# One core, two row tiles: tile 1's last products ordered behind tile 0's, a shorter log1p, and a memory projection that is recorded earlier

## The chip, the core and the metric

The kernel runs on one core of a Trainium2 chip. The metric is the device time of one execution in microseconds (us). A core has five engines that run their own instruction streams side by side: PE (TensorE, matrix products; its weight loads are listed apart as PEld), DVE (VectorE), ACT (ScalarE), POOL (GpSimd) and SP (SyncE, which here issues nearly all of the DMA transfers). They meet only at semaphores.

## The reference

A sequence of 256 rows of width 1024 goes through two blocks of two layers each, everything in float32. Cut to what the change touches:

```
# block 1
for layer in range(2):
    hn  = rmsnorm(h, gains[0])
    mix = mixer_ab(hn, ...) if layer == 0 else mixer_c(hn, ...)   # delta rule + mLSTM | windowed attention
    h   = h + rmsnorm(mix, gains[1])
    ff  = square(relu(rmsnorm(h, gains[2]) @ w_up[layer])) @ w_down[layer]
    h   = h + rmsnorm(ff, gains[3])
    h   = h + sigmoid(h @ w_ple_gate[layer]) * (p[layer] @ w_ple[layer])
# block 2
for layer in range(2):
    # five groups of heads, one of them attends to a memory of 256 rows:
    # its keys and values are rmsnorm(memory) @ w_k[layer], which needs nothing of h
    h = h + mixers(rmsnorm(h), memory) @ w_out[layer]
    h = h + (silu(rmsnorm(h) @ fg[layer]) * (rmsnorm(h) @ fu[layer])) @ fd[layer]
```

`softplus` in `mixer_ab` and `log_sigmoid` in both blocks need `log1p(exp(-|y|))`.

## The kernel before

**Tiles and precision.** The 256 rows are two tiles of 128, t = 0 and t = 1. Every weight matrix comes in blocks of up to 1 MB into one of two `raw` buffers. A block is then split into a high and a low part (`hi<-raw`, mostly on ACT, some on DVE; `lo<-raw,hi` on DVE), in four buffers of `hi` and four of `lo` (`NHL = 4`). A product of float32 accuracy is three PE products: activations high by weight high, high by low, low by high (`nmm`, for outputs with rows on the partitions; `tmm` for transposed outputs). Accumulators are PSUM banks of 512 columns, `ps` in the profile; tile t's result of 1024 columns takes two banks.

**Streams.** `stream` walks over a list of (block, tile) pairs. `lagged(n, lag)` lets tile 1 follow tile 0 by some blocks; `tail_lagged(n, tail)` interleaves the tiles block by block and then does the last `tail` blocks of tile 0 ahead of those of tile 1. At the last block of a tile it calls `done`, which starts a chain on DVE and ACT: for an output projection the sum of squares, the norm and the residual add into `h0` or `h1`, then transposes on PE (`ps<-cf,h`, `ps<-cf,w`) of the new rows, which the next matrix needs as its operand. `w0o` and `w1o` are the output projections of block 1's mixers, `wu`/`wd` the two matrices of its feed-forward (`ff1`), `wg` the gate that follows it, `wi` and `wm` the input projections of block 2's mixers, `wk` the memory's keys and values, `wo` the output projections, `fg`, `fu`, `fd` block 2's feed-forward (`ff2`).

**What sets the order.** No engine call is made at once. A `Recorder` notes all operations of the program with their tiles, derives the dependences from them, gives each a price in nanoseconds from a table, and lists them by a planner that follows the dependences (`order`, `arrange`, `tails`); then each engine's instructions are issued in that order, which the chip keeps. `LAG[a][b]` is the table's delay from an operation of engine a to a dependent one of engine b. `op.preds` are an operation's predecessors. The recording order itself (which the `Loom`, a set of generators, weaves) breaks ties and sets which buffer a tile gets. All of it is recorded by one line, so the profile shows every instruction under L613.

**Where the memory stands.** `memory_rms()` computes the norm of the memory's rows, `memory(0, memory_T(0))` streams the two 1 MB blocks of `wk0` (48 products of 512 columns) and starts the norm and the transposes of the keys. In the kernel before, both are recorded behind block 1's last feed-forward, `ff1(1, ...)`, and ahead of block 2's first mixers.

**log1p.** In `gates` (once, 128x256) and in `forget` (once a layer of block 2, 8 columns) log1p(e) is ln(u) · e / (u − 1) with u = e + 1, and e where u − 1 rounds to zero: seven DVE operations behind the `Ln`, a `RECIPROCAL` among them.

Of the kernel before, what the change touches and what calls it, by code (L numbers as in the profile page):

```python
# [257 lines left out]
class Recorder:  # L258
# [7 lines left out]
           "act": {"pe": 271, "act": 160, "dve": 142, "pool": 155, "sp": 1220},  # L266
           "dve": {"pe": 270, "act": 128, "dve": 127, "pool": 155, "sp": 1220},
           "pool": {"pe": 200, "act": 90, "dve": 69, "pool": 97, "sp": 1220},
           "sp": dict.fromkeys(("pe", "act", "dve", "pool", "sp"), 2050)}

    def __init__(self, nc):
        self.engines = {"pe": nc.tensor, "act": nc.scalar, "dve": nc.vector, "pool": nc.gpsimd, "sp": nc.sync}
        self.ops, self.pools, self.tile_pool, self.seen = [], {}, {}, {}
        self.run = None


    @contextmanager
    def together(self, share=1):

        self.run = []  # L280
        yield
        op = self.ops[self.run[0]]
        op.cost = op.cost / share + 200 * (share > 1)
        self.run = None

    def engine(self, name):
        rec = self
# [53 lines left out]
    def note(self, eng, call, args, kwargs):  # L341
        op = Op()
        op.eng, op.call, op.args, op.kwargs = eng, call, args, kwargs
        op.preds, op.succs, op.tiles, op.alt, op.more = {}, [], [], None, []
        op.table = self.TABLES.get(args[2], 0) if call == "activation" and args[2] != AF.Copy else None
        isap = lambda x: hasattr(x, "tensor") or hasattr(x, "tag_meta")
        outs = [kwargs[k] for k in ("out", "accum_out") if k in kwargs and isap(kwargs[k])]
        ins = [v for k, v in kwargs.items() if k not in ("out", "accum_out") and isap(v)]
        rest = [a for a in args if isap(a)]
        if "out" not in kwargs:  # L350
            outs.append(rest.pop(0))
        op.cost, op.lag = self.price(op, outs[-1], rest + ins), self.LAG[eng]
        if self.run:
            i = self.run[0]
            first = self.ops[i]
            first.more.append((call, args, kwargs))
            first.cost += op.cost
            op = first
        else:
            i = len(self.ops)  # L360
            self.ops.append(op)
            if self.run is not None:
                self.run.append(i)
        for x, write in [(x, False) for x in rest + ins] + [(x, True) for x in outs]:
            for b in self.boxes(x):
                self.touch(i, op, b, write)
# [294 lines left out]
def program(ctx, tc, A, out, dbg=None):  # L661
# [157 lines left out]
    def stream(name, items, acts, kpb, halves_, n, seq, done, before=None):  # L819
# [3 lines left out]
        for t in range(2):  # L823
            for i, tt in seq:
                if tt == t:
                    first.setdefault((items[i][0], t), i)
                    last[items[i][0], t] = i
        banks, live = {}, {}
        w = halves_ * n
        for i, t in seq:  # L830
            c, b, k0 = items[i]
# [5 lines left out]
                banks[c, t] = [acc() for _ in range(halves_)]  # L837
            hi, lo = live[i]
            for j in range(kpb):
                nmm(banks[c, t], acts(t, k0 + j), hi[:, j, :], lo[:, j, :],  # L840
                    first[c, t] == i and j == 0, last[c, t] == i and j == kpb - 1, n)
                if (j + 1) * 3 * halves_ % 6 == 0:
                    loom.step()
            if last[c, t] == i:
                done(c, t, banks.pop((c, t)))

    def a_T(t, k):
# [251 lines left out]
    def mixer_ab(end):  # L1099
        nab = gain(14)  # L1100
        done = {}
        st = {}

        def gates(bank):
# [6 lines left out]
            act.activation(e, e, AF.Exp)  # L1111
            dve.tensor_scalar(u, e, 1.0, None, op0=OP.add)
            act.activation(ln, u, AF.Ln)
            dve.tensor_scalar(u, u, -1.0, None, op0=OP.add)
            dve.scalar_tensor_tensor(z, u, 0.0, e, op0=OP.is_equal, op1=OP.mult)
            dve.tensor_scalar(u, u, 1e-30, None, op0=OP.max)
            dve.reciprocal(u, u)
            dve.tensor_tensor(ln, ln, e, op=OP.mult)
            dve.tensor_tensor(ln, ln, u, op=OP.mult)
            dve.tensor_tensor(ln, ln, z, op=OP.add)  # L1120
            dve.scalar_tensor_tensor(ln, y, 0.0, ln, op0=OP.max, op1=OP.add)
            ca = small(1)
            act.activation(ca, col("alog"), AF.Exp)
# [314 lines left out]
            loom.join(*([("B", j - 2)] if j >= 2 else [("A", j, t)]))  # L1438

        items = [(0, j, 2 * j) for j in (2, 3, 0, 1)]  # L1440
        stream("w0o", items, lambda t, k: done[k // 2, t](k % 2), 2, 2, 512, tail_lagged(4, 2), end, before)


    def mixer_c(r, end):
# [32 lines left out]
        def nat_done(c, t, banks):  # L1477
# [2 lines left out]
        items = [(c, 2 * c + i, 4 * i) for c in (2, 0, 1) for i in range(2)]  # L1480
        stream("w1n", items, a_T, 4, 1, 512, lagged(6, 2), nat_done)
        items = [(0, j, 2 * j) for j in range(4)]
        stream("w1o", items, lambda t, k: done[k // 2, t](k % 2), 2, 2, 512, tail_lagged(4, 2), end,
               lambda it, t: loom.join(("C", it[1], t)))


# [209 lines left out]
    def mixers2(l, r, e, mem, tab, lam, end):  # L1696
# [70 lines left out]
        def forget():  # L1767
# [5 lines left out]
            act.activation(e, e, AF.Exp)  # L1773
            dve.tensor_scalar(u, e, 1.0, None, op0=OP.add)
            act.activation(ln, u, AF.Ln)
            dve.tensor_scalar(u, u, -1.0, None, op0=OP.add)
            dve.scalar_tensor_tensor(z, u, 0.0, e, op0=OP.is_equal, op1=OP.mult)
            dve.tensor_scalar(u, u, 1e-30, None, op0=OP.max)
            dve.reciprocal(u, u)
            dve.tensor_tensor(ln, ln, e, op=OP.mult)  # L1780
            dve.tensor_tensor(ln, ln, u, op=OP.mult)
            dve.tensor_tensor(ln, ln, z, op=OP.add)
            dve.scalar_tensor_tensor(lg, y, 0.0, ln, op0=OP.min, op1=OP.subtract)
            yield
            yield
# [292 lines left out]
    def out1(c, t, banks):  # L2078
# [3 lines left out]
            g2.append(gain(6))  # L2082
        loom.spawn(pre_ff1(1, t, banks, g1[0], g2[0], e, gbo[0]), ("pre", 1, t))

    mixer_c(rc, out1)
    loom.drain()
    dumph("m1")
# [8 lines left out]
        yield from scaled_T(t, gi[0], ri, ei)  # L2096

    ff1(1, e, per_layer_input(1), into2)
    memory_rms()
    mem = memory(0, memory_T(0))  # L2100
    tab, lam = rope_tables2(0)
    loom.drain()
    dumph("f1")
# [57 lines left out]
```

## Time and profile before

| | |
|---|---|
| runs, median (lowest to highest) | 1399.25 us (1395.28 to 1400.75), 3 runs |
| the profiled execution | 1395.2 us, of which the span of the profile is 1393.4 us |
| mean granted clock of TensorE | 0.996 |
| busy share of the span | PE 98%, PEld 86%, DVE 72%, ACT 56%, POOL 4% |
| DMA | 236.36 MB, mean 170 GB/s |

The profile is of one execution; its span leaves 1.8 us of the execution's time outside. An engine's idle time stands in brackets behind the instruction that ended it, with what released it. An operation's row in the timeline has its start, its busy time and how many equal ones followed one another; products are pipelined, so they start closer together than they last.

### The profile page before, as it was taken

The numbers are of one execution on the slowest core, as the hardware profiler recorded it, in microseconds if no ns is written. First come the engines' busy times: TensorE is split into PE (matmuls) and PEld (weight loads), VectorE is DVE, ScalarE is ACT, GpSimd is POOL, SyncE is SP. The second block draws the span as 40 slices with busy tenths as digits, with TensorE's granted clock in tenths as the row PEclk, the third lists the DMA queues.
The fourth block names the chain that finished last, engine by engine and source line by source line (L and its number), as shares of the span: only waits on it lengthen the run. The fifth ranks groups of instructions, "written<-read, shape, count | busy, mean of one in ns | idle before, by whom it ended". The sixth has DMA issues, their size and how long they took to land.

```text
span 1393.4 us, 23108 instructions
## 1 busy us (share of the span) xinstructions
PE 1359.3 (98%) x8768; PEld 1199.4 (86%) x8774; DVE 998.3 (72%) x2417; ACT 786.4 (56%) x1800; POOL 56.4 (4%) x93
## 2 busy tenths in 40 slices
PE   6999999999999999999999999999999999999998
PEld 6899889999787799998787877999998877899997
DVE  6994876666677876566789798575767999576664
ACT  6665554444554854445576596454546679364443
POOL 0000210000010010000020000000001000000000
PEclk9999999999999999999999999999999999999999
DMA  8332354445543364445555243454545523345553
GB/s 329 134 126 99 114 212 182 182 184 194 212 147 141 139 224 179 185 182 194 207 193 206 91 142 132 152 211 153 212 155 205 187 90 99 144 153 210 182 189 114
DMA packets 36400, 236.36 MB, mean 170 GB/s; under 512 B 4160, under 2 KB 4416, under 8 KB 10176
## 3 DMA queue, kind: packets, MB, share of 16 engines
q1 hardware_dynamic: 36288, 234.88, 46.4%
q8 instruction: 69, 1.13, 0.3%
q14 instruction: 43, 0.35, 0.1%
HBM read 233.82 MB, written 1.05 MB: 169 GB/s over the span
## 4 chain that ended last, share of the span: by engine, by line
PE 88%; DVE 6%; ACT 4%; issue 1%; DMA 1%; SPq 0%; POOLq 0%; POOL 0%; ACTq 0%; DVEq 0%
PE ps L613 88%; ACT w L613 3%; DVE w L613 3%; DVE s L613 2%; DMA cf<-in_cf 1%; DVE lo L613 1%; ACT hi L613 1%; DVE h L613 0%; ACT L613 0%; SPq L613 0%; POOLq L2157 0%; DVE hi L613 0%; ACT aTh L613 0%; POOL s L613 0%; ACTq L613 0%
## 5 line engine op out<-in xcount | busy, mean ns | idle before, releaser
L613 ACT ACTIVATE hi<-raw 128x512 fp32r<-128x512 f32 (+1 forms) x793 | 437.6, 620 | 297.7 <-PE ps L613 244.9
L613 DVE TENSOR_TENSOR lo<-raw,hi 128x512 fp32r<-128x512 f32 (+1 forms) x844 | 526.0, 678 | 51.4 <-ACT hi L613 48.1
L613 PE MATMUL ps<-hi,w 128*128 128x512 f32 (+1 forms) x1272 | 379.1, 395 | 0.5 <-ACT w L613 0.5
L613 PE MATMUL ps<-aTl,hi 128*128 128x256 f32 x1256 | 316.7, 280 | 0.0
L613 PE MATMUL ps<-aTh,hi 128*128 128x256 f32 x1256 | 316.3, 281 | 0.0
L613 PE MATMUL ps<-aTh,lo 128*128 128x256 f32 x1256 | 312.5, 280 | 0.0
L613 PEld LDWEIGHTS ps<-hi,w 128*128 128x128 f32 x1272 | 225.2, 188 | 36.1 <-issue 1.9
L613 PEld LDWEIGHTS ps<-aTh,hi 128*128 128x128 f32 x1256 | 224.8, 188 | 9.4 <-ACT hi L613 0.4
L613 PEld LDWEIGHTS ps<-aTl,hi 128*128 128x128 f32 x1256 | 225.1, 188 | 8.3 <-issue 0.4
L613 PEld LDWEIGHTS ps<-aTh,lo 128*128 128x128 f32 x1256 | 223.6, 189 | 9.9 <-DVE lo L613 1.0
L613 PE MATMUL ps<-lo,w 128*128 128x512 f32 (+1 forms) x636 | 205.9, 393 | 0.0
L613 ACT ACTIVATE w<-ps 128x512 f32<-128x512 f32 (+3 forms) x261 | 128.3, 535 | 130.4 <-PE ps L613 119.9
L613 PE MATMUL ps<-hi,aTh 128*128 128x512 f32 (+2 forms) x480 | 148.4, 366 | 3.7 <-ACT w L613 2.5
L613 DVE CAST hi<-raw 128x512 fp32r<-128x512 f32 x51 | 21.8, 427 | 177.8 <-PE ps L613 177.8
L613 PE MATMUL ps<-lo,aTh 128*128 128x512 f32 (+2 forms) x480 | 147.2, 365 | 0.0
L613 PE MATMUL ps<-hi,aTl 128*128 128x512 f32 (+2 forms) x480 | 147.2, 365 | 0.0
L613 ACT ACTIVATE w<-w 128x512 fp32r<-128x512 f32 (+5 forms) x143 | 74.9, 535 | 95.3 <-DVE w L613 93.0
L613 PEld LDWEIGHTS ps<-lo,w 128*128 128x128 f32 x636 | 112.6, 188 | 17.0 <-issue 0.8
L613 PE MATMUL ps<-cf,w 128*128 128x128 f32 (+1 forms) x572 | 94.7, 279 | 17.4 <-DMA cf<-in_cf 10.6
L613 PE MATMUL ps<-w,w 128*64 128x128 f32 (+10 forms) x912 | 109.5, 299 | 0.6 <-ACT w L613 0.5
L613 PEld LDWEIGHTS ps<-w,w 128*128 128x128 f32 (+4 forms) x912 | 88.7, 171 | 20.0 <-ACT w L613 7.4
L613 PEld LDWEIGHTS ps<-hi,aTh 128*128 128x128 f32 x480 | 86.8, 190 | 16.2 <-ACT w L613 2.8
(105 smaller groups left out, 1143.8 us busy)
## 6 DMA issues: line engine op xcount, KB each, us to landing
raw<-in_wu SPq DMA_DIRECT2D x32, 1024.0 KB, 4.8
raw<-in_wd SPq DMA_DIRECT2D x32, 1024.0 KB, 5.0
raw<-in_fg SPq DMA_DIRECT2D x22, 1024.0 KB, 4.8
raw<-in_fu SPq DMA_DIRECT2D x22, 1024.0 KB, 4.8
raw<-in_fd SPq DMA_DIRECT2D x22, 1024.0 KB, 4.8
raw<-in_wi SPq DMA_DIRECT2D x20, 1024.0 KB, 4.8
raw<-in_w0t SPq DMA_DIRECT2D x10, 1024.0 KB, 5.5
raw<-in_wo SPq DMA_DIRECT2D x10, 1024.0 KB, 4.8
```

What stands on the lines that cost most here:

```text
L613: getattr(self.engines[op.eng], call)(*args, **kwargs)
```

## The change

Five edits:

- In the table of delays, the delay from one SP operation to a dependent SP operation becomes 0 instead of 2050.
- `stream`, where it has just two accumulations (one for each tile): when tile 0's last product has been recorded, its number is kept (`ended`), and all products of tile 1 recorded later get it as an additional predecessor (`rec.behind(..., only="pe")`). Both lie on PE, so no semaphore and no instruction is added; the planner may only not place them earlier.
- log1p: four DVE operations in place of seven, ln(u) + (u − 1 − e)(0.5 e − 1).
- `w0o` and `w1o`: `tail_lagged(4, 3)` in place of `tail_lagged(4, 2)`.
- `memory_rms()` and `mem = memory(0, memory_T(0))` are recorded ahead of `mixer_c`, layer 1's attention, instead of behind `ff1(1, ...)`.

```diff
-           "sp": dict.fromkeys(("pe", "act", "dve", "pool", "sp"), 2050)}
+           "sp": {"pe": 2050, "act": 2050, "dve": 2050, "pool": 2050, "sp": 0}}
...
+    @contextmanager
+    def behind(self, *ops, only=None):
+
+        self.hold, self.only = ops, only
+        yield
+        self.hold = ()
+
+    def last(self):
+        return len(self.ops) - 1
...
             self.ops.append(op)
+            if self.hold and self.only in (None, eng):
+                op.preds.update(dict.fromkeys(self.hold, True))
...
             for j in range(kpb):
-                nmm(banks[c, t], acts(t, k0 + j), hi[:, j, :], lo[:, j, :],
-                    first[c, t] == i and j == 0, last[c, t] == i and j == kpb - 1, n)
+                with rec.behind(*(ended if t else ()), only="pe"):
+                    nmm(banks[c, t], acts(t, k0 + j), hi[:, j, :], lo[:, j, :],
+                        first[c, t] == i and j == 0, last[c, t] == i and j == kpb - 1, n)
...
             if last[c, t] == i:
+                if t == 0 and len(last) == 2:
+                    ended.append(rec.last())
                 done(c, t, banks.pop((c, t)))
...
             act.activation(ln, u, AF.Ln)
-            dve.tensor_scalar(u, u, -1.0, None, op0=OP.add)
-            dve.scalar_tensor_tensor(z, u, 0.0, e, op0=OP.is_equal, op1=OP.mult)
-            dve.tensor_scalar(u, u, 1e-30, None, op0=OP.max)
-            dve.reciprocal(u, u)
-            dve.tensor_tensor(ln, ln, e, op=OP.mult)
-            dve.tensor_tensor(ln, ln, u, op=OP.mult)
-            dve.tensor_tensor(ln, ln, z, op=OP.add)
+
+            dve.scalar_tensor_tensor(u, u, -1.0, e, op0=OP.add, op1=OP.subtract)
+            dve.tensor_scalar(z, e, 0.5, -1.0, op0=OP.mult, op1=OP.add)
+            dve.tensor_tensor(u, u, z, op=OP.mult)
+            dve.tensor_tensor(ln, ln, u, op=OP.add)
...
-        stream("w0o", items, lambda t, k: done[k // 2, t](k % 2), 2, 2, 512, tail_lagged(4, 2), end, before)
+        stream("w0o", items, lambda t, k: done[k // 2, t](k % 2), 2, 2, 512, tail_lagged(4, 3), end, before)
...
+    memory_rms()
+    mem = memory(0, memory_T(0))
     mixer_c(rc, out1)
...
     ff1(1, e, per_layer_input(1), into2)
-    memory_rms()
-    mem = memory(0, memory_T(0))
     tab, lam = rope_tables2(0)
```

The order is what the edits change on the chip. PE at the end of layer 0's feed-forward, before. `ps445` and `ps446` are the two banks of tile 0's `wd0` result, `ps447` and `ps448` those of tile 1, `hi`/`lo` the halves of its weights, `w` its activations; the products with `h1` and `h0` are the transposes of the new rows of tile 1 and tile 0, and those with `aTh` belong to the gate `wg0`, whose operand they make:

```order
L613 MATMUL ps447_539<-lo634_726,w627_719 128x512
L613 MATMUL ps447_539<-hi633_725,w628_720 128x512
L613 MATMUL ps445_537<-hi633_725,w627_719 128x512
L613 MATMUL ps446_538<-hi633_725,w627_719 128x512
L613 MATMUL ps445_537<-lo634_726,w627_719 128x512
L613 MATMUL ps445_537<-hi633_725,w628_720 128x512
L613 MATMUL ps446_538<-lo634_726,w627_719 128x512
L613 MATMUL ps446_538<-hi633_725,w628_720 128x512
L613 MATMUL ps652_744<-cf_76,h1_82 128x128 x4
L613 MATMUL ps653_745<-cf_76,h1_82 128x128 x4
L613 MATMUL ps643_735<-cf_76,h0_81 128x128 x4
L613 MATMUL ps665_757<-hi655_747,aTh_84 128x512
```

Here tile 1's last product stands six ahead of tile 0's last, and behind tile 0's last there is nothing but the transposes that need both.

The same place after, first where tile 0 ends (its last product is the one on `ps445` with `w628`), then, 32 products of tile 1 further on, where its transposes stand:

```order
L625 MATMUL ps448_540<-hi608_700,w595_687 128x512
L625 MATMUL ps446_538<-hi633_725,w628_720 128x512
L625 MATMUL ps445_537<-hi633_725,w628_720 128x512
L625 MATMUL ps447_539<-hi619_711,w605_697 128x512
L625 MATMUL ps448_540<-hi619_711,w605_697 128x512
```

```order
L625 MATMUL ps448_540<-hi633_725,w627_719 128x512
L625 MATMUL ps643_735<-cf_76,h0_81 128x128 x4
L625 MATMUL ps447_539<-lo634_726,w627_719 128x512
L625 MATMUL ps448_540<-lo634_726,w627_719 128x512
L625 MATMUL ps447_539<-hi633_725,w628_720 128x512
L625 MATMUL ps448_540<-hi633_725,w628_720 128x512
L625 MATMUL ps644_736<-cf_76,h0_81 128x128 x4
L625 MATMUL ps658_750<-hi655_747,aTh_84 128x512
L625 MATMUL ps658_750<-lo656_748,aTh_84 128x512
L625 MATMUL ps657_749<-hi655_747,aTh_84 128x512
L625 MATMUL ps657_749<-lo656_748,aTh_84 128x512
```

Tile 0's last product now stands ahead of 32 products of tile 1, which are what PE does until the transposes of `h0`, and four more products of tile 1 stand between those. The first transposes of `h1` stand behind 16 products of the gate of tile 0. The end of layer 1's feed-forward changes in the same way, with 32 products of tile 1 behind tile 0's last and 21 products of the gate and four transposes ahead of those of `h1`.

SP, the queue that issues the DMA transfers, around the memory's blocks, before (`memT` and `memx` are the memory's rows, transposed and plain, `wg1` layer 1's gate, `wi00` the first input projection of block 2):

```order
L613 DMA w1224_1318<-in_memT 128x512
L613 DMA raw1178_1270<-in_wg1 128x2048
L613 DMA w1227_1321<-in_memT 128x512
L613 DMA gb1950_2044<-in_gb 128x1024
L613 DMA w1206_1298<-in_memx 128x512
L613 DMA raw1274_1368<-in_wi00 128x1424
L613 DMA raw1231_1325<-in_wk0 128x2048
L613 DMA raw1278_1372<-in_wi00 128x1424
L613 DMA w1207_1299<-in_memx 128x512
L613 DMA raw1235_1329<-in_wk0 128x2048
L613 DMA w1212_1305<-in_memx 128x512
L613 DMA w1213_1306<-in_memx 128x512
```

After, the four `memT` transfers stand at queue rows 32 to 37, in layer 0, one `memx` at row 40, and the rest here (`wg0` is layer 0's gate, `w1n` layer 1's attention projection):

```order
L625 DMA raw659_751<-in_wg0 128x2048
L625 DMA w694_786<-in_memx 128x512
L625 DMA w699_792<-in_memx 128x512
L625 DMA w700_793<-in_memx 128x512
L625 DMA raw662_754<-in_wg0 128x2048
L625 DMA raw667_759<-in_wg0 128x2048
L625 DMA gb745_839<-in_gb 128x1024
L625 DMA raw764_858<-in_w1n 128x2048
L625 DMA raw718_812<-in_wk0 128x2048
L625 DMA raw752_846<-in_w1n 128x2048
L625 DMA raw722_816<-in_wk0 128x2048
L625 DMA raw769_863<-in_w1n 128x2048
```

So the blocks of `wk0` are now fetched between those of `w1n` and no longer between those of `wi00`, and their 48 products stand on PE within layer 1's attention.

## Rows read from the trace of the kernel before

**Rows 1.** The page: span, busy times, one costly group (busy us, mean ns).

```profile
span 1393.4 us, 23108 instructions
...
PE 1359.3 (98%) x8768; PEld 1199.4 (86%) x8774; DVE 998.3 (72%) x2417; ACT 786.4 (56%) x1800; POOL 56.4 (4%) x93
...
L613 DVE TENSOR_TENSOR lo<-raw,hi 128x512 fp32r<-128x512 f32 (+1 forms) x844 | 526.0, 678 | 51.4 <-ACT hi L613 48.1
```

**Rows 2.** The waits of PE: total us, times, longest.

```profile
PE ps L613 <- DMA cf<-in_cf: 10.6, 1, 10.6
PE ps L613 <- ACT w L613: 6.6, 13, 2.5
...
PE ps L613 <- issue: 3.8, 4, 3.3
```

**Rows 3.** Timeline of PE, end of layer 0's feed-forward.

```profile
375.76 0.84 PE L613 MATMUL ps<-hi,w 128*128 128x512 f32 x3
...
377.12 0.39 PE L613 MATMUL ps<-hi,w 128*128 128x512 f32 x1
380.86 2.79 PE L613 MATMUL ps<-cf,h 128*128 128x128 f32 x12 [3.35 <-issue]
```

**Rows 4.** Timeline of PE, end of layer 1's feed-forward.

```profile
680.09 0.39 PE L613 MATMUL ps<-hi,w 128*128 128x512 f32 x1
683.89 2.79 PE L613 MATMUL ps<-cf,h 128*128 128x128 f32 x12 [3.41 <-DVE h L613]
```

**Rows 5.** Stretches behind both: length, PE, PEld, DVE, ACT, POOL, granted clock, DMA.

```profile
381.00:384.00 3.00, 3.00 (x14) 2.90 (x15) 2.94 (x5) 1.92 (x4) 0.16 (x1) 0.50 0.45 162
384.00:388.00 4.00, 4.00 (x16) 3.25 (x15) 3.26 (x6) 2.44 (x5) 0.00 (x0) 0.69 0.00 0
684.00:688.00 4.00, 4.00 (x21) 3.77 (x22) 3.58 (x7) 2.90 (x7) 0.15 (x1) 0.65 0.49 187
```

**Rows 6.** Timeline of PE, end of `w0o`.

```profile
187.52 0.39 PE L613 MATMUL ps<-hi,w 128*128 128x512 f32 x1
...
195.14 0.63 PE L613 MATMUL ps<-cf,w 128*128 128x128 f32 x4 [1.79 <-DVE w L613]
```

**Rows 7.** Timeline of DVE in `gates`.

```profile
51.79 1.73 DVE L613 RECIPROCAL w<-w 128x256 f32<-128x256 f32 x1
53.45 0.35 DVE L613 SCALAR_TENSOR_TENSOR w<-w 128x256 f32<-128x256 f32 x1
53.73 0.40 DVE L613 TENSOR_TENSOR w<-w,w 128x256 f32<-128x256 f32 x1
```

**Rows 8.** Timeline of PE behind `gates`.

```profile
59.93 1.13 PE L613 MATMUL ps<-w,cf 128*128 128x256 f32 x4 [0.87 <-ACT w L613]
```

**Rows 9.** Stretches of layer 1's attention, then of block 2's first mixers.

```profile
440.00:450.00 10.00, 9.84 (x71) 7.18 (x70) 10.00 (x24) 5.58 (x18) 0.00 (x0) 1.00 0.13 52
450.00:460.00 10.00, 9.54 (x73) 6.01 (x70) 10.00 (x56) 10.00 (x52) 0.00 (x0) 1.00 0.01 2
460.00:470.00 10.00, 9.38 (x77) 7.18 (x78) 10.00 (x38) 7.96 (x31) 0.15 (x1) 1.00 0.29 95
...
730.00:760.00 30.00, 27.32 (x125) 22.44 (x124) 28.13 (x110) 20.11 (x43) 0.27 (x1) 1.00 0.56 205
...
788.00:850.00 62.00, 60.42 (x438) 46.08 (x440) 59.72 (x226) 58.59 (x183) 1.68 (x7) 1.00 0.31 103
```

**Rows 10.** Timeline around 755 us in block 2's first mixers: PE.

```profile
759.56 0.50 PE L613 MATMUL ps<-hi,aTh 128*128 128x512 f32 x1 [2.52 <-ACT w L613]
```

**Rows 11.** The same place on ACT.

```profile
752.69 2.20 ACT L613 ACTIVATE hi<-raw 128x512 fp32r<-128x512 f32 x4 [2.70 <-DMA raw<-in_wi]
```

**Rows 12.** Timeline of all engines where `fg0` gets a weight buffer.

```profile
949.87 1.68 ACT L613 ACTIVATE hi<-raw 128x512 fp32r<-128x512 f32 x3 [4.44 <-PE ps L613]
949.87 0.43 DVE L613 CAST hi<-raw 128x512 fp32r<-128x512 f32 x1 [5.17 <-PE ps L613]
...
950.47 0.33 PE L613 MATMUL ps<-aTh,hi 128*128 128x256 f32 x1
```

More of the change, by code (lines that the diff above doesn't have):

```diff
@@ L273, in __init__ @@
         self.ops, self.pools, self.tile_pool, self.seen = [], {}, {}, {}
-        self.run = None
+        self.run, self.hold = None, ()
     @contextmanager
@@ L827, in stream @@
                     last[items[i][0], t] = i
-        banks, live = {}, {}
+        banks, live, ended = {}, {}, []
         w = halves_ * n
@@ L1482, in mixer_c @@
         items = [(0, j, 2 * j) for j in range(4)]
-        stream("w1o", items, lambda t, k: done[k // 2, t](k % 2), 2, 2, 512, tail_lagged(4, 2), end,
+        stream("w1o", items, lambda t, k: done[k // 2, t](k % 2), 2, 2, 512, tail_lagged(4, 3), end,
                lambda it, t: loom.join(("C", it[1], t)))
@@ L1775, in forget @@
             act.activation(ln, u, AF.Ln)
[L1776 to L1782, printed above, removed]
+            dve.scalar_tensor_tensor(u, u, -1.0, e, op0=OP.add, op1=OP.subtract)
+            dve.tensor_scalar(z, e, 0.5, -1.0, op0=OP.mult, op1=OP.add)
+            dve.tensor_tensor(u, u, z, op=OP.mult)
+            dve.tensor_tensor(ln, ln, u, op=OP.add)
             dve.scalar_tensor_tensor(lg, y, 0.0, ln, op0=OP.min, op1=OP.subtract)
```

## The prediction

> **What bounds the kernel now.** I read the busy times first, then the waits of PE, then the timeline of PE around each long wait, and last the tables by stretch. PE is busy 1359.3 of 1393.4 us [rows 1], so only 34.1 us are to be had from waits, plus whatever PE does at a lower clock. The largest wait is the first load, 10.6 us [rows 2], which no edit touches. The next are two of 3.35 and 3.41 us, at the ends of block 1's two feed-forwards [rows 3, 4]. In the list of waits [rows 2] the first stands under "issue" (3.8 in all, longest 3.3); its place in the order shows that it is a wait of the same kind as the second, whose releaser is `DVE h`: PE stands before the transposes of the new rows until DVE has added and normed them. Behind both the granted clock is low: 0.50 and 0.69 over 7 us, and 0.65 over 4 us, with PE busy throughout [rows 5]. In 0.50 TensorE runs at its 1.2 GHz level, else at 2.4; the other two values are means of both. Some 13 short waits for `ACT w` make up 6.6 us [rows 2], the longest of 2.52 us in block 2's first mixers [rows 10]. Over long stretches DVE is the fuller engine: 59.72 of 62 us with PE at 60.42 [rows 9].
>
> **The change part by part.** A positive term is time saved, against the profiled execution's 1395.2 us (span 1393.4 and 1.8 outside it). Products follow one another every 0.225 us: three take 0.84 where one takes 0.39 [rows 3].
>
> *A, the ends of the feed-forwards.* The predecessors put on tile 1's products of the gate force the planner to finish tile 0 of the gate first, and that needs `h0` early; so the end of `wd` is turned round, as the order shows. Before, tile 1's last product starts at 375.76 and ends at 376.15, and its transposes start at 380.86: a chain of 4.7 us. Tile 0's ends at 377.51 and its transposes stand behind eight of the twelve that take 2.79 us, so they start at 382.7 at the latest: at most 5.2 us [rows 3]. In layer 1, tile 1's last product stands eight ahead of the one at 680.09, ends near 678.7 and its transposes start at 683.89: 5.2 us [rows 4]. After, tile 0's chain has 32 products behind it, 32 × 0.225 = 7.2 us, more than 5.2: no wait. Tile 1's chain has 16 products of the gate and four transposes (about 0.5): 4.1 us, so 0.6 to 1.1 are left, I take 0.8. In layer 1 it has 21 products and four transposes, 5.2: nothing left. The waits give 3.35 + 3.41 − 0.8 = 6.0. The lower clock behind them costs, as time lost from full speed, 3 × 0.50 + 4 × 0.31 + 4 × 0.35 = 4.1 [rows 5]. A wait of 1.79 us elsewhere [rows 6] is not among the stretches with a low clock, so the 0.8 that is left should not bring it back. A = +10.1. Upper end 10.9, without the 0.8. Lower end: the chain at `w0o` takes 7.2 us (below); if these take as long when DVE has more to do, 3.1 and 2.0 us are left and only 1.7 of the waits goes, and the clock's 4.1 is in doubt: +1.7.
>
> *B, `w0o` and `w1o`.* At `w0o` tile 0's last product ends at 187.91 and its transposes start at 195.14, 7.2 us, with a wait of 1.79 [rows 6]. Between them PE does 24 products before and 27 after (counted in the two orders): 3 × 0.225 = +0.7. The predecessor does little here: of a tile's two banks only the second's last product is the held one, and tile 1's products do not move behind both (six before, five after). At `w1o` nothing waits now. Bounds 0 to 1.8.
>
> *C, log1p.* Removed: a reciprocal with 1.66 us from its start to the next [rows 7], and six operations; added: four. The rest are 0.28 to 0.33 apart [rows 7], so DVE's chain shrinks by 1.66 + 2 × 0.3 = 2.3 us. On the path it can give no more than the wait that hangs on it, 0.87 [rows 8], since PE has products of the projection to do until then: +0.8, bounds 0 and 0.9. In `forget`, 8 columns wide, no wait of PE hangs on it: 0.
>
> *D, the memory's products in layer 1's attention.* 48 products, 48 × 0.225 = 10.8 us of PE work, come to where PE idles 0.16 + 0.46 + 0.62 = 1.24 us while DVE is full [rows 9]. With them come eight `lo` splits, 8 × 0.68 = 5.4 us of DVE [rows 1], and eight `hi` splits, 8 × 0.55 = 4.4 of ACT [rows 11], less than PE gets, so they do not make DVE the longer one by themselves. +1.2; bounds −2 (the splits land in the stretch with DVE at 10.00 of 10) and +1.2. SP's transfers collide with little: the core's DMA share is 0.01 to 0.29 there [rows 9].
>
> *E, the place the products leave.* At 759.56 PE waits 2.52 us for the split of a `wi` block [rows 10], which ACT began late because the block's transfer landed late, 2.70 us of waiting for `raw<-in_wi` [rows 11]. The two `wk0` blocks no longer stand in the same two `raw` buffers and the same queue. +2.5; bounds 0 and 2.5.
>
> *F, block 2's first attention.* PE arrives some 11 us earlier, with 5.4 us less for DVE to do, in a stretch where DVE works 28.13 of 30 and then 59.72 of 62 us [rows 9]. PE may find DVE behind by up to 10.8 − 5.4 = 5.4 us, or the 1.58 it idles there may shrink. Nearer to even, since between the two DVE has room: +0.5, bounds −5.4 and +1.6.
>
> *G, new short waits.* Where the order changes, new waits of the common kind come up: 12 waits for `ACT w` other than the longest make 4.1 us [rows 2], 0.34 each; I take four: −1.4, bounds −4 and 0.
>
> The delay of SP in the planner's table moves nothing by itself on the chip: 0. Sum: 10.1 + 0.7 + 0.8 + 1.2 + 2.5 + 0.5 − 1.4 = 14.4, so 1380.8 for an execution like the profiled one. That one lies 4.05 us below the median of the runs; against the median the forecast is 1384.9, **1385**.
>
> **The rivals.** *The chain is longer than its cover.* The edit of `stream` holds tile 1 well only where a result is a single bank, and turning the two ends round helps only if the chain from last product to transposes is near 5 us. Against: both rows say 4.7 to 5.2 [rows 3, 4], with both tiles' chains in flight at once. For: 7.2 at `w0o` [rows 6]. Then A is 1.7 to 5.8 and the sum 6 to 10: 1389 to 1393.
>
> *The memory's move only shifts cover.* D and E come to nothing and F to −4: 14.4 − 1.2 − 2.5 − 4.5 = 6.2, 1393, within what the measurement tells from no change. For it: DVE at 28.13 of 30 us just where PE will now be early [rows 9].
>
> *Slower: the weight buffers run out.* The next layer's `wk1` blocks now hold two of the four `hi`/`lo` buffers through `ff2(0)` where one was held, so later blocks are split just ahead of use. Counted in the two orders, ten blocks have their first product 0.8 to 1.2 us of PE work behind the last use of their buffer, four before. What speaks against: at `fg0` a copy starts at 949.87, on the release, takes 0.43 on DVE, and the block's first product starts at 950.47, 0.60 us later, with no idle time of PE at it [rows 12]. But ACT runs copies in rows of four that last 2.20 us [rows 11]; a copy that stands behind such a row is late by 2.20 less a margin of some 0.4, 1.8 at a place, 18 at ten: 1385 + 18 = 1403, slower than before. It decides from 1.4 us at a place on, where all of the sum is used up. The Trainium skill (Perfetto Trace Analysis, Identifying Performance Opportunities) reads evenly repeated bubbles on the engine that should be full as a sign that memory for the next tile may be short, which speaks against an edit that ties buffers up. By that rule the time would be this rival's 1403, by [rows 12] nothing is lost, and the row decides.
>
> **How the numbers follow.** What a measurement of this kernel tells from no change is about 0.5%, 7.0 us: faster is below 1392.3, slower above 1406.3. Chances: the forecast, 1380 to 1388, 0.60; the longer chain 0.17, of which 0.12 is faster; the shifted cover 0.10, of which 0.02 is faster; the buffers 0.07, of which 0.04 is above 1406 (more places or longer rows of copies than reckoned); and 0.06 that waits in the two attentions go which I did not count, 1372 to 1380. Faster 0.60 + 0.12 + 0.02 + 0.06 = 0.80, same 0.16, slower 0.04. The range 1374 to 1394 leaves out the buffers and a rest of the others, together some 0.15.
>
> **What would show it.** A: no wait of over 1.2 us ahead of `ps<-cf,h` at the two ends, and clock 1.0 behind them. B: a wait near 1.1 where 1.79 stood. C: less than 0.3 where 0.87 stood. D and F: the idle time of PE in the two attentions, 1.24 and 1.58 before. E: no wait for `raw<-in_wi` on ACT in block 2's first mixers. The buffers: waits of PE for `ACT hi` or `DVE lo` spread over `ff2(0)`. The prediction is wrong if the waits at the two ends stay above 2 us with a low clock behind, or if the first attention of block 2 loses what they give.

## The result and the profile after

The changed kernel takes 1383.37 us in the median (1382.09 to 1383.89, 4 runs), the kernel before in the same comparison 1397.84 (1395.28 to 1400.75, 4 runs). The ratio is 0.9895, with a 95% interval of 0.9872 to 0.9917: 14.5 us less by the medians, clear of noise. The forecast was 1385, between 1374 and 1394. One execution of one kernel below (log1p alone) took 2733.01 us, about twice all the others, and is left out. The profiled execution after took 1383.1 us with a span of 1381.3, 12.1 less than the span before [rows 1].

The page after, its head and busy times:

```profile
span 1381.3 us, 23088 instructions
...
PE 1356.1 (98%) x8767; PEld 1195.3 (87%) x8774; DVE 1002.5 (73%) x2422; ACT 786.7 (57%) x1794; POOL 47.4 (3%) x85
```

PE does the same products, and is idle for 25.2 us where it was for 34.1 [rows 1]; its busy time is 3.2 shorter. So of the 12.1 us, 8.9 are waits and 3.2 are the same work done in less time, most of it the clock (4.1 us lost to it before by [rows 5], 4 × 0.37 = 1.5 after, below). The waits of PE after, in total, times and longest:

```profile
PE ps L625 <- DMA cf<-in_cf: 11.1, 1, 11.1
PE ps L625 <- DVE w L625: 4.8, 4, 2.9
PE ps L625 <- ACT w L625: 1.9, 4, 0.9
PE ps L625 <- DVE aTl L625: 1.6, 2, 1.4
```

Against [rows 2], both waits of over 3 us at the ends of the feed-forwards are gone, and `ACT w` falls from 6.6 to 1.9. One new long wait is there, 2.9 us for `DVE w`. The end of layer 0's feed-forward after, in the timeline of PE:

```profile
376.81 0.60 PE L625 MATMUL ps<-cf,h 128*128 128x128 f32 x4
377.16 0.72 PE L625 MATMUL ps<-lo,w 128*128 128x512 f32 x2
377.72 0.63 PE L625 MATMUL ps<-hi,w 128*128 128x512 f32 x2
378.19 0.60 PE L625 MATMUL ps<-cf,h 128*128 128x128 f32 x4
...
382.33 0.27 PE L625 MATMUL ps<-cf,h 128*128 128x128 f32 x1
```

The transposes of tile 0 now stand between products of tile 1, and those of tile 1 at 382.33 between products of the gate, without a bracket anywhere: PE waits for none of them, where [rows 3] had 3.35. Behind the two ends the clock is full (columns as in [rows 5]):

```profile
376.00:388.00 12.00, 12.00 (x59) 9.33 (x58) 12.00 (x23) 8.88 (x20) 0.77 (x2) 1.00 0.67 250
688.00:700.00 12.00, 12.00 (x58) 9.70 (x57) 7.80 (x13) 5.82 (x11) 0.55 (x1) 1.00 0.61 218
```

The new wait stands at the last output projection, `wo1`. Timeline of PE there, after:

```profile
1186.53 0.39 PE L625 MATMUL ps<-hi,w 128*128 128x512 f32 x1
1189.85 1.94 PE L625 MATMUL ps<-cf,w 128*128 128x128 f32 x8 [2.94 <-DVE w L625]
```

and the table by stretch behind it:

```profile
1190.00:1194.00 4.00, 3.95 (x21) 3.52 (x21) 3.54 (x6) 2.25 (x5) 1.32 (x2) 0.63 0.04 14
```

The same place before, in the timeline of PE:

```profile
1199.04 0.39 PE L613 MATMUL ps<-hi,w 128*128 128x512 f32 x1
1200.97 1.29 PE L613 MATMUL ps<-cf,w 128*128 128x128 f32 x8 [1.54 <-DVE w L613]
1202.78 0.39 PE L613 MATMUL ps<-hi,aTh 128*128 128x256 f32 x1 [0.52 <-ACT aTh L613]
...
1204.07 1.32 PE L613 MATMUL ps<-cf,w 128*128 128x128 f32 x8 [0.56 <-DVE w L613]
```

and its stretch:

```profile
1202.00:1206.00 4.00, 2.92 (x20) 2.06 (x19) 3.55 (x7) 2.90 (x6) 1.23 (x1) 1.00 0.02 4
```

Before, PE waited 1.54, 0.52 and 0.56 us, 2.62 in all, at full clock. After it waits 2.94 us in one piece and the clock behind it is 0.63 for 4 us. The change makes this one place worse, though by less than the two figures suggest: from the start of the last product of `wo1` (1199.04 before, 1186.53 after) to the end of the span it takes 194.4 us before and 194.8 after.

### The profile page after: what moved, and what is told of

It is laid out like the page before. It is cut to its first block, busy times and chain, and to the rows that moved or that the text cites. A ratio compares the mean times of both kernels' runs of the same rounds, so it can differ in the third digit from the quotient of the medians.

```text
span 1381.3 us, 23088 instructions
## 1 busy us (share of the span) xinstructions
PE 1356.1 (98%) x8767; PEld 1195.3 (87%) x8774; DVE 1002.5 (73%) x2422; ACT 786.7 (57%) x1794; POOL 47.4 (3%) x85
## 3 DMA queue, kind: packets, MB, share of 16 engines
HBM read 233.82 MB, written 1.05 MB: 170 GB/s over the span
## 4 chain that ended last, share of the span: by engine, by line
PE 85%; DVE 10%; DMA 2%; ACT 2%; issue 1%; POOL 0%; SPq 0%; ACTq 0%; DVEq 0%
PE ps L625 85%; DVE lo L625 4%; DVE w L625 3%; DVE s L625 2%; DMA raw<-in_w0t 2%; ACT w L625 1%; ACT hi L625 1%; DMA raw<-in_wp 0%; DMA raw<-in_wu 0%; DVE h L625 0%; ACT L625 0%; DVE aTl L625 0%; POOL s L625 0%; DVE tab L625 0%; DVE hi L625 0%
## 5 line engine op out<-in xcount | busy, mean ns | idle before, releaser
L625 PE MATMUL ps<-aTh,hi 128*128 128x256 f32 x1256 | 334.0, 281 | 0.1
L625 PE MATMUL ps<-aTl,hi 128*128 128x256 f32 x1256 | 332.0, 280 | 0.2 <-DVE aTl L625 0.2
L625 PE MATMUL ps<-aTh,lo 128*128 128x256 f32 x1256 | 331.7, 280 | 0.3 <-DVE lo L625 0.2
L625 PE MATMUL ps<-lo,w 128*128 128x512 f32 x636 | 214.5, 395 | 0.0
L625 ACT ACTIVATE w<-ps 128x512 f32<-128x512 f32 (+2 forms) x261 | 125.8, 511 | 116.3 <-PE ps L625 110.0
L625 PE MATMUL ps<-hi,aTh 128*128 128x512 f32 (+2 forms) x480 | 162.0, 373 | 1.5 <-DVE w L625 0.6
L625 PE MATMUL ps<-lo,aTh 128*128 128x512 f32 (+2 forms) x480 | 162.0, 370 | 0.4 <-DVE lo L625 0.4
L625 PE MATMUL ps<-hi,aTl 128*128 128x512 f32 (+2 forms) x480 | 159.3, 366 | 0.0
L625 ACT ACTIVATE w<-w 128x512 f32<-128x512 f32 (+5 forms) x144 | 75.6, 533 | 106.0 <-DVE w L625 103.6
L625 PEld LDWEIGHTS ps<-cf,w 128*128 128x128 f32 (+1 forms) x572 | 72.9, 144 | 31.9 <-DVE w L625 13.2
```

The lines of the kernel that those rows point to most:

```text
L625: getattr(self.engines[op.eng], call)(*args, **kwargs)
```

## The experiments

Four kernels undo or do the parts, four vary the predecessors, four price single questions. Ratios are against the kernel before, measured beside each. Its own median lies between 1395.91 and 1398.4 us in these comparisons, so a difference between two changed kernels is known to some 2 us at best, and is given by ratios too where it matters.

### The predecessors alone

```diff
# kernel before, with
+                with rec.behind(*(ended if t else ()), only="pe"):
...
+                    ended.append(rec.last())
```

> The kernel before with the predecessors of tile 1's products alone. Theory (the waits at the ends of block 1's two feed-forwards went because these predecessors turn the end of wd round): both waits of 3.35 and 3.41 us are gone and the clock behind them is 1.0, so 10 to 12 us faster than before; the wait of 2.52 us in block 2's first mixers stays. Rival (what made room is the memory's work taken out from behind the second feed-forward): the second wait stays, 5 us faster at most.

Measured: 1387.63 us, ratio 0.9931 (0.9911 to 0.9951), 8.6 us less. Both waits at the ends are gone, so the theory holds there and the rival falls; the gain is below the 10 to 12 expected. The wait of 2.52 us in block 2's first mixers is gone too, which I had not expected: between 700 and 800 us PE's only wait left is one of 0.7. And `w0o` has become slower, which takes part of the gain. Its waits in the timeline of PE:

```profile
189.62 0.73 PE L625 MATMUL ps<-hi,w 128*128 128x512 f32 x2 [0.66 <-ACT hi L625]
194.15 1.26 PE L625 MATMUL ps<-cf,w 128*128 128x128 f32 x8 [1.71 <-DVE w L625]
196.01 0.69 PE L625 MATMUL ps<-cf,w 128*128 128x128 f32 x2 [0.61 <-DVE w L625]
```

2.98 us in three pieces, where [rows 6] has 1.79 in one. Behind the last products of tile 0 stand 19 products ahead of its transposes, in place of 24 (counted in the two orders).

### The memory's move alone

```diff
# kernel before, with
+    memory_rms()
+    mem = memory(0, memory_T(0))
     mixer_c(rc, out1)
```

> The kernel before with only the memory's norm and projection recorded ahead of layer 1's attention. Theory: both waits of over 3 us at the ends of the feed-forwards stay with their low clock; what goes is the wait of 2.52 us and part of the idle time in the two attentions: 2 to 4 us faster. Rival (the cover that the products give up is needed where they stood): no change within 1 us or slower, with new waits around the first mixers of block 2.

Measured: 1389.44 us, ratio 0.9942 (0.9924 to 0.9959), 6.8 us less: more than the theory's 2 to 4. The ends of the feed-forwards are as before or worse. The timeline of PE at the two:

```profile
382.00 2.79 PE L613 MATMUL ps<-cf,h 128*128 128x128 f32 x12 [3.13 <-issue]
...
693.64 2.79 PE L613 MATMUL ps<-cf,h 128*128 128x128 f32 x12 [4.22 <-DVE h L613]
```

The wait of 2.52 us is gone here as well, and in layer 1's attention, in the 35 us from 435 on, PE is busy 34.68 instead of 33.77 us. The profile of this run has a span of 1388.9, only 4.5 below that before, so part of the 6.8 may be the spread between executions.

### log1p alone

```diff
# kernel before, in gates and forget
-            dve.reciprocal(u, u)
...
+            dve.scalar_tensor_tensor(u, u, -1.0, e, op0=OP.add, op1=OP.subtract)
```

> The kernel before with the short log1p alone. First theory (the prediction's): the wait of 0.87 us behind the gates goes, 0.8 us faster. Second theory, from the profile after, where PE lost no time less in that stretch: PE comes to another wait on the same chain or on a table load of ACT, and the time stays within 0.5 us of before at that place; a larger difference can only come from products that the planner puts elsewhere.

Measured: 1395.64 us (median of nine), ratio 0.9987 (0.9975 to 1.0), no gain that this measurement separates from none. No row of its trace is read.

### All but the predecessors

```diff
# changed kernel, with
-                with rec.behind(*(ended if t else ()), only="pe"):
+                with rec.behind(*(()), only="pe"):
```

> The changed kernel without the predecessors (all else kept, the two lists with three blocks in the tail too). Theory: the two waits of over 3 us return with a low clock behind them, 10 to 12 us slower than the changed kernel, so 1 to 3 us faster than before. Rival (the edits overlap, any of them shortens the ends): less than 5 us slower than the changed kernel.

Measured: 1392.05 us, ratio 0.997 (0.9959 to 0.9982), so 8.7 us over the changed kernel by medians and 10.5 by ratios, where 10 to 12 were expected. Both waits return, 3.13 and 3.42 us. A low clock returns only behind the second. The first in the timeline of PE, then the stretches behind the first and behind the second:

```profile
379.54 1.95 PE L625 MATMUL ps<-cf,h 128*128 128x128 f32 x12 [3.13 <-issue]
```

```profile
379.00:383.00 4.00, 3.38 (x22) 2.69 (x23) 4.00 (x7) 3.89 (x10) 0.84 (x1) 1.00 0.42 131
...
690.00:694.00 4.00, 4.00 (x19) 3.70 (x18) 3.58 (x7) 2.72 (x5) 0.00 (x0) 0.50 0.32 111
```

Without predecessors the tail of three and the planner's new delay change nothing: the instructions of every engine and their order are those of the second experiment's kernel with the short log1p. It is not faster than that one; its ratio is the higher of the two, with intervals that just touch, and the spans of the two profiles are alike, 1388.6 and 1388.9. With the predecessors in, the new delay was not tried by itself.

### Predecessors at the gates only

```diff
# changed kernel, with
-                if t == 0 and len(last) == 2:
+                if t == 0 and len(last) == 2 and name.startswith("wg"):
```

> The changed kernel with the predecessors only at the two gates wg0 and wg1. Theory A (the prediction's: the gate's predecessors turn the end of wd round): no wait of over 1.2 us at the ends of the feed-forwards, and the 10 to 12 us of those two places are kept; w0o loses its 1.1 us. Theory B (any predecessors behind the feed-forward make tile 0's chain the longer one for the planner, the gate's are not needed): the same here. Apart from these places within 3 us of the changed kernel.

Measured: 1383.3 us, ratio 0.9906 (0.9891 to 0.9921). No wait of PE is listed between 360 and 400 us and only one of 0.2 between 660 and 700. The gate's predecessors suffice for the two ends. `w0o` has waits of 1.28, 0.39 and 0.32, some 1.5 us more than the changed kernel's single 0.45, near the 1.1 expected.

### Predecessors everywhere but at the gates

```diff
# changed kernel, with
-                if t == 0 and len(last) == 2:
+                if t == 0 and len(last) == 2 and not name.startswith("wg"):
```

> The changed kernel with the predecessors everywhere but at the gates. Theory A: the two waits of over 3 us come back, 10 us slower than the changed kernel. Theory B: the end of wd is turned round all the same, the wait ahead of the transposes of tile 0 is gone; the first transposes of tile 1 stand behind 10 and 12 products, 2.3 and 2.7 us, less than the chain of 4.7 to 5.2, so that waits of 2 to 3 us remain there, 3 to 6 us slower than the changed kernel.

Measured: 1384.54 us, ratio 0.9914 (0.9899 to 0.9929). Theory A falls: the end of `wd` is turned round all the same. The timeline of PE at the two ends:

```profile
377.36 1.03 PE L625 MATMUL ps<-cf,h 128*128 128x128 f32 x8
379.27 0.50 PE L625 MATMUL ps<-hi,aTh 128*128 128x512 f32 x1 [0.87 <-ACT aTh L625]
381.02 0.51 PE L625 MATMUL ps<-hi,aTl 128*128 128x512 f32 x1 [0.57 <-DVE aTl L625]
...
685.37 0.60 PE L625 MATMUL ps<-cf,h 128*128 128x128 f32 x4
686.02 0.60 PE L625 MATMUL ps<-cf,h 128*128 128x128 f32 x4
687.67 0.50 PE L625 MATMUL ps<-hi,aTh 128*128 128x512 f32 x1 [1.05 <-ACT aTh L625]
```

The transposes of tile 0 stand ahead of the gate and wait for nothing; what is left is 0.87 + 0.57 and 1.05 us behind them, less than the 2 to 3 of theory B, and the clock stays at 1.00 in both stretches. So the kernel is only 1.2 us over the changed one by medians, 2.7 by ratios, where theory B had 3 to 6.

### A tail of two at `w0o` and `w1o`

```diff
# changed kernel, with
-        stream("w0o", ..., tail_lagged(4, 3), end, before)
+        stream("w0o", ..., tail_lagged(4, 2), end, before)
# and the same at w1o
```

> The changed kernel with two blocks in the tail at w0o and w1o again. The kernel before with the predecessors alone lost 3.4 us at w0o against before. Theory (with a tail of two the predecessors take away cover at w0o, and the third block gives it back): the same loss here, 4 to 5 us slower than the changed kernel, all of it in the 15 us around the end of w0o. Rival (that loss came from the long log1p and what it delayed): within 1.5 us of the changed kernel.

Measured: 1387.97 us, ratio 0.9939 (0.9923 to 0.9956), 4.6 us over the changed kernel by medians, 6.2 by ratios. At `w0o` the same three waits as in the first experiment are back: 0.66, 1.70 and 0.61. With 2.97 us of waits for 0.45, and a clock of 0.59 in the 4 us from 198 on, some 4 us are lost there. The theory holds for this place, with the short log1p in the kernel, and the rival falls; that all of the loss lies there is not shown, since the two profiles are 6.6 us apart.

### Both banks held, a tail of three in block 2 too

```diff
# changed kernel, with
-                    ended.append(rec.last())
+                    ended.extend(rec.last() - q for q in range(halves_))
...
-        stream(f"wo{l}", ..., tail_lagged(5, 2), end,
+        stream(f"wo{l}", ..., tail_lagged(5, 3), end,
```

> The changed kernel with both banks of tile 0 as predecessors, not only the second, and with three blocks in the tail of block 2's output projections too. Theory (the waits left ahead of the transposes at the four output projections, 0.45, 1.4, 0.5 and 2.9 us, come from too few products of tile 1 behind tile 0's last): these waits shrink by 3 to 5 us in all, 1378 to 1381 us. Rival (they are held by DVE's and ACT's queues, or more products behind only delay tile 0's last): within 2 us of the changed kernel, 1381 to 1385.

Measured: 1378.16 us (1377.4 to 1378.44), ratio 0.9866 (0.985 to 0.9883): below both kernels, the changed one by 5.2 us by medians and 4.1 by ratios, with intervals that overlap a little. Of the 5.0 us of waits at the four output projections of the changed kernel (0.45, 1.37, 0.24 and 2.94) 1.4 are left (none, none, 0.53 and 0.89). Timeline of PE at `wo1`:

```profile
1187.41 0.39 PE L625 MATMUL ps<-hi,aTh 128*128 128x256 f32 x1 [0.67 <-ACT aTh L625]
1188.14 0.38 PE L625 MATMUL ps<-hi,aTl 128*128 128x256 f32 x1 [0.22 <-DVE aTl L625]
```

The stretch behind it:

```profile
1190.00:1194.00 4.00, 4.00 (x37) 4.00 (x36) 4.00 (x7) 3.50 (x9) 0.00 (x0) 1.00 0.00 0
```

0.89 us of waits for 2.94, and the clock at 1.00. The last product of `wo1` starts at 1185.68, and the span ends at 1376.7: 191.0 us for this part, where the changed kernel takes 194.8.

### Both banks held, tails as in the change

```diff
# changed kernel, with
-                    ended.append(rec.last())
+                    ended.extend(rec.last() - q for q in range(halves_))
```

> The changed kernel with both banks as predecessors and the tails of block 2's output projections left at two. The version with both edits came to 1378.16 us. Theory (the longer tail shortens the waits at wo, both banks those at w0o and w1o): 1 to 3 us faster than the changed kernel, the wait of 2.9 us with the low clock behind it at the last output projection stays. Rival (both banks suffice): 1378 to 1379 us, that wait gone too.

Measured: 1379.99 us, ratio 0.9876 (0.9855 to 0.9898), 3.4 us below the changed kernel by medians, 2.7 by ratios, again with intervals that overlap. At `wo1` only 0.25 and 0.58 are left. The rows there, in the timeline of PE:

```profile
1187.20 0.39 PE L625 MATMUL ps<-hi,w 128*128 128x512 f32 x1
1187.43 1.03 PE L625 MATMUL ps<-cf,w 128*128 128x128 f32 x8
1188.71 0.39 PE L625 MATMUL ps<-hi,aTh 128*128 128x256 f32 x1 [0.25 <-ACT aTh L625]
...
1190.04 0.39 PE L625 MATMUL ps<-hi,aTl 128*128 128x256 f32 x1 [0.58 <-DVE aTl L625]
```

So holding the other bank too suffices there, and the theory's half on `wo1` falls. From the last product of `wo1` to the end of the span it takes 191.9 us, 2.9 less than the changed kernel. In the order, 26 products stand between tile 0's last product and its transposes, in place of 8. But the output projection of block 2's first layer has a wait of 1.37 at 852 us, which the tail of three does not show. The remaining 1.8 us between the two versions are within what their intervals leave open.

### Three weight buffers

```diff
# changed kernel, with
-NHL = 4
+NHL = 3
```

> The changed kernel with three instead of four hi and lo buffers (NHL = 3), which makes every weight block be split later. It prices the rival that weight buffers held by wk1 run out. Theory (margins of 0.8 us cost nothing, PE's products hide the splits as long as the first copy starts on the release): less than 5 us slower than the changed kernel, none of it as a repeated wait over ff2(0). Rival (the buffers are what keeps PE full): over 15 us slower, with waits for ACT hi and DVE lo at nearly every block.

Measured: 1393.52 us, ratio 0.9973 (0.9961 to 0.9985), about 10 us over the changed kernel: between the two expectations, and for the most part at another place than the rival names. Over `ff2(0)` PE has one wait, of 0.4 us:

```profile
868.00:1050.00 182.00, 182.00 (x1322) 170.91 (x1323) 118.34 (x227) 90.99 (x174) 0.00 (x0) 1.00 0.50 184
```

Some 7 of the 10 us are lost in layer 0's delta rule; the rest was not traced to a place. About the same number of products there takes 30 us, of which PE is busy 26.59, against 23 in the changed kernel (the first row is of this kernel, the second of the changed one):

```profile
70.00:100.00 30.00, 26.59 (x200) 25.27 (x199) 29.16 (x104) 17.03 (x32) 0.00 (x0) 0.94 0.37 134
```

```profile
69.00:92.00 23.00, 23.00 (x202) 22.95 (x201) 22.72 (x80) 15.13 (x30) 0.00 (x0) 1.00 0.38 133
```

### The memory where it was

```diff
# changed kernel, with
-    memory_rms()
-    mem = memory(0, memory_T(0))
     mixer_c(rc, out1)
...
     ff1(1, e, per_layer_input(1), into2)
+    memory_rms()
+    mem = memory(0, memory_T(0))
```

> The changed kernel with the memory's norm and projection recorded behind ff1(1) again. Theory (the move gave 1 to 4 us in layer 1's attention and little elsewhere; the wait of 2.52 us in block 2's first mixers went through the new order, since it was gone with the predecessors alone): 1 to 4 us slower than the changed kernel, the wait for a block of wi does not return. Rival (the move gives what it gave alone in the second run, 6 to 8 us, on top): 6 us slower or more.

Measured: 1380.51 us, ratio 0.9883 (0.9861 to 0.9905), beside the changed kernel's 0.9895: no slower; its profiled span is 3.5 us shorter. Neither expectation of a loss came true. The wait for a block of `wi` does not return (PE has one wait between 695 and 855 us, 0.6 for `DVE aTl`), and the 1.37 at `w1o` is not there.

### The long log1p

```diff
# changed kernel, with
-            dve.scalar_tensor_tensor(u, u, -1.0, e, op0=OP.add, op1=OP.subtract)
...
+            dve.reciprocal(u, u)
```

> The changed kernel with the long log1p. First theory (the prediction's): 0.8 us slower, in the stretch from 50 to 66 us. Second theory (its path ends in a wait of another kind that takes its place): within 0.5 us in that stretch.

Measured: 1381.87 us, ratio 0.9889 (0.9868 to 0.9911): no slower. Behind the gates it has the old wait, the changed kernel another one in its place (timeline of PE; first this kernel, then the changed one):

```profile
60.01 1.13 PE L625 MATMUL ps<-w,cf 128*128 128x256 f32 x4 [0.87 <-ACT w L625]
```

```profile
60.97 0.33 PE L625 MATMUL ps<-cf,w 128*128 128x128 f32 x1 [1.08 <-DVE w L625]
```

## Why the prediction was right

**A, the ends of the feed-forwards: right, at its upper end.** Forecast +10.1, with 0.8 us of wait left. Nothing is left, and the clock behind is 1.00, so the rows of before are all given back: 3.35 + 3.41 + 4.1 = 10.9. The 4.1 of the clock belongs to that one execution: in the fourth experiment the first wait is back with 3.13 us, and the clock behind it is 1.00. The 0.8 was too careful because the chain of tile 1 became shorter: its last product starts at 377.95 (the second of the pair at 377.72), ends at 378.35, and its transposes at 382.33 find no wait, so it takes at most 4.0 us where 4.7 was read off [rows 3]. That the two tiles' chains no longer run at the same time on DVE and ACT would explain it; no run separates that. *The step that named the cause was too narrow.* The prediction put the turning of `wd` down to the predecessors at the gate. They do suffice (fifth experiment), but it is turned as well with predecessors everywhere else and none at the gates (sixth), and not without any (fourth). What can be said is that either set makes the planner end tile 0 first; that predecessors on later products lengthen tile 0's remaining path in its reckoning is my reading of the code, not shown by a run. Which of the predecessors away from the gates does it in the sixth was not tried.

**B, `w0o` and `w1o`: the sum nearly right, the reasons not.** At `w0o` +0.7 was forecast and the wait goes from 1.79 to 0.45, +1.3. "The predecessor does little here" was wrong: with a tail of two it costs, 2.98 us of waits for 1.79 (first and seventh experiments), and the tail of three is what turns the loss into a gain: 19 products stand behind tile 0's last one with a tail of two, 27 with three, 24 before. Without predecessors the tail of three does nothing, the order is the same. The bank that is not held ends only five products ahead of tile 1; with both held 38 products stand behind tile 0's last, and PE waits for none of its transposes there (ninth experiment). At `w1o`, where nothing waited, 1.37 us appeared. That is not owed to the hold alone: 1.17 us are there without any predecessor (fourth experiment), and nothing with the hold and the memory where it was (eleventh). The rows of the changed kernel at both, in the timeline of PE:

```profile
197.29 0.39 PE L625 MATMUL ps<-hi,aTh 128*128 128x256 f32 x1 [0.45 <-ACT aTh L625]
...
504.80 1.09 PE L625 MATMUL ps<-cf,w 128*128 128x128 f32 x8 [1.37 <-DVE aTl L625]
```

**C, log1p: wrong.** +0.8 was forecast. The 0.87 goes, but PE waits 1.08 us at the transposes just behind, which start at 60.97; before they followed at 60.90 without a wait, and by two experiments the edit is worth nothing that can be told from nothing. The bound of 0 held. The step that failed was to take a wait's length for the gain without asking what stands behind it on the same chain.

**D, E, F, the memory's move: +4.2 forecast, not owed to the move.** Most of the gains are there in the trace, but they do not hang on the move of the products. In layer 1's attention (D) PE idles 0.32 us between 440 and 470, where it idled 1.24. The wait of 2.52 us (E) goes with the predecessors alone, with the move alone, and stays away when the memory is put back. On ACT four waits of 7.2 us in all for `raw<-in_wi` are still there between 690 and 800 us, against what the prediction said would show E; PE seems to have enough ahead of them. Between 700 and 860 us PE waits 1.8 us instead of 4.1. Alone the move is worth 0.58%, on top of the rest nothing that the intervals show: the parts remove in part the same waits, the 2.52 at least, and do not add up. Why the small waits come and go with each listing stays open.

**G, new short waits: −1.4, with one large one missed.** The sum is near: 1.37 at `w1o` and some below 1 us in block 2. What was missed is `wo1`, not in the prediction at all: 2.62 us of waits at full clock became 2.94 with 4 us at 0.63, 0.3 + 4 × 0.37 = 1.8 us if both are added. Net, the two profiles lose 0.4 us there, 194.8 for 194.4 from the last product to the end, and part of the clock's share belongs to this execution (last section). The prediction had noted at `w0o` that only the second bank is held and that tile 1's products therefore do not move behind both; it took this for no effect. Between tile 0's last product and its transposes stand 9 products before, 8 after and 26 with both banks held, where the waits shrink to 0.83 and the part behind becomes 2.9 us shorter. So the hold on one bank gave no cover here, and the second gives it, shown by the ninth experiment. That the wait grew is not owed to that hold alone: without any predecessor (fourth experiment) it is 2.62 in one piece, and why is open.

**The rivals.** The longer chain did not come: the chain shrank. The buffers did not run out: `ff2(0)` has no wait of PE in the changed kernel, and with a buffer less a single one of 0.4. With three buffers most of the loss lies in the delta rule, where 200 products took 30 us instead of 23, with three waits of 0.75 to 1.50 for `DVE w` and `ACT w`, and with a clock of 0.94. The Trainium skill (Perfetto Trace Analysis, Identifying Performance Opportunities) names evenly repeated bubbles as a possible sign of too little room for the next tile; no run here shows such a row of bubbles, also with less room. The shifted cover came in part: on top of the rest D, E and F are worth nothing, but F does not lose the 4 us that it named.

The sum of the forecast, 14.4, and the 12.1 us between the two profiles thus agree for partly wrong reasons: A carries 10.9 of it; C and the move's own share were counted too high, and `wo1` was not counted. That 1385 came within 1.6 us of 1383.37 is luck in part. The sum alone gives 1380.8 for the profiled execution, which took 1383.1, 2.3 more; the 4.05 added for the profiled execution of before, which lay that far below its median, went the other way, since that of after lies 0.3 below its own.

## What to carry to other kernels

Where two tiles go through the same stages, look in the order for where each ends: what counts is how much independent work stands behind a tile's last product, against the length of the chain from there to its transposes. A planner can be made to end one tile first by predecessors on its own engine, which add no product and no copy; but hold all accumulators of the tile, and give the tail enough blocks, or the hold takes away the cover that it should make (2.98 us for 1.79 here, and 4 to 5 us gained when both were put right). In a kernel whose order is planned as a whole, waits of half a microsecond, here up to 1.4, move with every edit: price an edit against the rest of the change, not against the kernel before alone.

## What was not expected of the hardware

The granted clock behind a wait did not follow from the wait's length. At `wo1` the changed kernel waits 2.94 us and the clock behind it is 0.63 over 4 us. The sixth experiment's kernel has the same products in the same order there and the same wait, and its clock stays at 1.00. Its timeline of PE, and the stretches from there on:

```profile
1191.43 1.29 PE L625 MATMUL ps<-cf,w 128*128 128x128 f32 x8 [2.94 <-DVE w L625]
```

```profile
1190.00:1194.00 4.00, 2.08 (x13) 1.49 (x14) 3.54 (x6) 3.27 (x7) 2.29 (x2) 1.00 0.40 166
1194.00:1198.00 4.00, 4.00 (x33) 3.63 (x34) 4.00 (x7) 1.20 (x2) 0.00 (x0) 1.00 0.02 4
```

The same 2.94 us stand at `wo1` in four more kernels: behind them the clock is low in the first, seventh and eleventh experiments (0.64, 0.58 and 0.63 over 4 us), and 1.00 in the twelfth. Shorter waits can be followed by a low clock too: with predecessors at the gates only, those at `wo1` were 1.49, 0.42 and 0.17 and the clock behind them 0.59, where the kernel before has 1.54, 0.52 and 0.56 and 1.00. The stretch of the kernel with predecessors at the gates only:

```profile
1190.00:1194.00 4.00, 3.83 (x20) 3.54 (x21) 3.38 (x7) 2.03 (x4) 0.43 (x1) 0.59 0.00 0
```

What decides it no run here separates. The mean granted clock also differs between executions of one and the same kernel: among 19 of the kernel before it goes from 0.999, in one of 1393.99 us, to 0.991, in one of 1401.06. So the time that the clock costs behind a wait, read off one profile, is a price of that execution, and not one that every execution pays.
